# Depthwise convolutions of a two-block network: matrix multiplies replaced by multiply-add instructions on VectorE

## The chip, the cores and the metric

The kernel runs as one program on one core of a Trainium2 chip. The core has a matrix engine (TensorE, PE in the profile), a vector engine (VectorE, DVE), a scalar engine (ScalarE, ACT), GpSimd (POOL) and SyncE (SP), whose queue issues nearly all transfers here. The engines run beside each other, each through its own list of instructions in a fixed order, and wait for each other on semaphores. The metric is the device time of one execution in microseconds (us), as the median of three runs.

## The reference

A state-space block over 256 tokens of width 1024 is followed by a two-layer block that works on two streams, the tokens `x` and a context of 256 tokens. The mixer of each layer has four branches: a Fourier mix, a convolution, grouped attention and differential attention. The convolution is the part that matters here; it is depthwise over tokens, 31 taps wide, on 512 channels:

```python
def conformer_conv(z, w, bias, ln_g, ln_b):
    a, g = jnp.split(z, 2, axis=-1)
    u = a * jax.nn.sigmoid(g)
    pad = CONV_KERNEL // 2                      # CONV_KERNEL = 31
    y = lax.conv_general_dilated(u, w[:, None, :], window_strides=(1,), padding=[(pad, pad)],
                                 dimension_numbers=("NWC", "WIO", "NWC"), feature_group_count=512) + bias
    return jax.nn.silu(layer_norm(y, ln_g, ln_b))
```

It is needed three times: in layer 0 for the context and for `x`, in layer 1 for `x` alone (the context is not updated in the last layer).

## The kernel before

Activations lie with the features on the 128 partitions and the 256 tokens along the free dimension. All large products are made in three multiplies of a rounded high part and a low part: for every weight tile, `wunits` loads 128x1024 values (`ws`), ScalarE casts them to the high part `wh` (L336), VectorE subtracts to get the low part `wl` (L337), and `mm3` (L358) issues 24 multiplies of 128x128 by 128x256 for it. There are four buffers each of `wh` and `wl`, so the split of a weight tile waits until TensorE has freed the buffer of an earlier one.

`conv_start` (L1043) makes the first half of the convolution branch. For each of four groups of 128 channels it multiplies the two input projections, and forms the gated input `up` with one ScalarE and one VectorE instruction (L1057, L1058), between zeros that POOL writes (L1054, L1055). The padded rows then go to DRAM (`du`) and come back as `ux`, a tile that holds 32 channels in four copies, each shifted by one token. With a table of diagonal 32x32 blocks (`cw`, loaded from `w_cv`), 32 matrix multiplies of 128x32 by 32x256 (L1070) sum the taps four at a time, and ScalarE adds the bias and writes `cy` (L1072). `conv_steps` (L1075) takes `cy` later: its first instruction, L1080, adds the four groups for the layer norm.

The calls are: L1701 for the context of layer 0, inside the first block; L1712 for `x` of layer 0, ahead of its `mixer`; L1739 for `x` of layer 1. In `mixer` (L1469) come the projections, grouped attention (`gqa_steps`), differential attention with the Fourier mix and the first gated branches beside it, and only then `conv_steps`, beside the branch `zd`. A softmax (L1295) is a chain of VectorE and ScalarE steps: the maximum of the scores (L1299), its scaling (L1300), the exponential on ScalarE (L1302), the reciprocal of the sum (L1304), the scaling of the probabilities (L1332 or L1368), which TensorE then transposes (L1312).

The order on each engine is made when the program is built. A list scheduler gives every instruction a priority, by default the place in which the code issues it, and puts those that are ready on their engines by priority. `high_priority(offset=...)` shifts the priority of what is issued inside it; a negative offset moves it back by so many places. The kernel has used that for the second block's modulation weights (`ada_next`, L973).

Of the kernel before, what the change touches and what calls it, by code (L numbers as in the profile page):

```python
# [9 lines left out]
F32 = mybir.dt.float32  # L10
F32R = mybir.dt.float32r
I32 = mybir.dt.int32
AF = mybir.ActivationFunctionType
ALU = mybir.AluOpType
# [3 lines left out]
P = 128  # L18
D = 1024
L = 256  # L20
# [11 lines left out]
def _vec_layout():  # L32
    off = 0
    for name, n in (
        ("norm_ffn", 8), ("norm_ple", 8), ("norm_final", 8), ("final_norm", 8),
        ("norm_mix2", 16), ("norm_ffn2", 16), ("b_ada", 96), ("c", 16),
        ("conv_b", 8), ("ln_g", 8), ("ln_b", 8), ("diff_norm", 2),
        ("qn", 128), ("kn", 128),
    ):
        VEC[name] = (off, n)  # L40
        off += n
    return off


NVEC = _vec_layout()

S5C = {}
# [17 lines left out]
def _cols(v):  # L65
    return np.asarray(v).reshape(-1, P).T


def _wfeat(w, cols_per_unit=1):

    k, m = w.shape
    return w.reshape(k // P, P, m // P, P).transpose(2, 1, 0, 3)


def host_layout(i):
    a = {k: np.asarray(v) for k, v in i.items()}
    o = {}
# [10 lines left out]
    def put(name, v, at=0):  # L88
        off, n = VEC[name]
        vec[:, off + at : off + at + v.shape[1]] = v  # L90
# [10 lines left out]
    put("ln_g", _cols(a["conv_ln_g_2"]))  # L101
    put("ln_b", _cols(a["conv_ln_b_2"]))
    put("diff_norm", a["diff_norm_2"].T)
    lam = np.stack([a["lam_q1_2"], a["lam_k1_2"], a["lam_q2_2"], a["lam_k2_2"]], axis=1)
    o["lam"] = np.broadcast_to(lam.reshape(1, 512), (P, 512))
    put("qn", np.broadcast_to(a["q_norm_2"].reshape(1, 128), (P, 128)))
# [51 lines left out]
    o["w_ada1"] = a["w_ada_2"][1].reshape(4, 2, P, 12, 512).transpose(3, 0, 2, 1, 4).reshape(48, P, 1024)  # L158
    wc = [_wfeat(w_in[l][:, 512:1536]).reshape(2, 4, P, 1024).transpose(1, 2, 0, 3) for l in range(2)]
    o["w_cin"] = np.stack(wc).reshape(8, P, 2048)  # L160

    cw = np.concatenate([a["conv_w_2"], np.zeros((2, 1, 512), np.float32)], axis=1).reshape(2, 8, 4, 4, 4, 32)
    cv = np.zeros((2, 4, 4, 32, 8, 4, 32), np.float32)
    e = np.arange(32)
    cv[:, :, :, e, :, :, e] = cw.transpose(5, 0, 3, 2, 1, 4)
    o["w_cv"] = cv.reshape(8, P, 1024)
    tok = np.concatenate([w_in[:, :, 0:512], w_in[:, :, 1536:3840]], axis=2)

    o["w_tok"] = tok[:, :, 1024:1280].reshape(2, 8, P, 256).transpose(0, 2, 1, 3).reshape(2, P, 2048)
# [18 lines left out]
    for l in range(2):  # L188
        w = _wfeat(a["w_ffn2_2"][l])
        for part in range(2):  # L190
            v = w[:, :, part * 8 : part * 8 + 8].reshape(4, 2, P, 1024)
# [9 lines left out]
    e = np.arange(64)  # L201
    an = 2.0 * np.pi * ((e[:, None] * e[None, :]) % 64) / 64
    bd = np.zeros((2, P, P))
    for h in range(2):
        q = slice(64 * h, 64 * h + 64)
# [78 lines left out]
class Net:  # L284
# [758 lines left out]
    def conv_start(self, l, h):  # L1043


        V, S, G, T = self.V, self.S, self.G, self.T
        y = self.k4([P, 4, L], F32, "cy")
        for k in range(4):
            ua, ug = self.wunits(self.a["w_cin"][l * 4 + k])
            ps = self.pm((P, 2, L))  # L1050
            self.mm3(ps[:, 0], ug, h, range(KC))
            self.mm3(ps[:, 1], ua, h, range(KC))
            up = self.up.tile([P, CW], F32, tag="up", bufs=2, name=self.nm("up"))
            G.memset(up[:, 0:15], 0.0)  # L1054
            G.memset(up[:, L + 15 : CW], 0.0)  # L1055
            t = self.k1([P, L])
            S.activation(t, ps[:, 0], AF.Tanh, scale=0.5)  # L1057
            V.scalar_tensor_tensor(up[:, 15 : 15 + L], t, 1.0, ps[:, 1], op0=ALU.add, op1=ALU.mult)  # L1058
            out = self.dr.tile([P, CW], F32, tag="du", name=self.nm("du"))
            self.nc.sync.dma_start(out, up)  # L1060
            sh = self.up.tile([P, 4, L + 28], F32, tag="ux", name=self.nm("ux"))
            v = out.rearrange("(q c) s -> c q s", c=32)
            for i in range(4):
                self.nc.sync.dma_start(sh[32 * i : 32 * i + 32], v[:, :, i : i + L + 28])
            w = self.k4([P, 8, 4, 32], F32, "cw")
            self.nc.sync.dma_start(w.rearrange("p j q c -> p (j q c)"), self.a["w_cv"][l * 4 + k])
            ps = self.px()
            for j in range(8):
                for q in range(4):
                    T.matmul(ps[32 * q : 32 * q + 32, :], w[:, j, q], sh[:, q, 4 * j : 4 * j + L],  # L1070
                             start=j == 0, stop=j == 7)
            S.activation(y[:, k], ps, AF.Identity, bias=self.cb2[:, l * 4 + k : l * 4 + k + 1])  # L1072
        return y

    def conv_steps(self, l, y, z):  # L1075
# [536 lines left out]
    def run(self):  # L1612
        tc, nc = self.tc, self.nc
        V, S, G = self.V, self.S, self.G
        with ExitStack() as st:
            def pool(name, bufs=1, es=st, **k):
                return es.enter_context(tc.tile_pool(name=name, bufs=bufs, **k))
# [3 lines left out]
            self.p1 = pool("p1")  # L1621
            self.p2 = pool("p2")
            self.p4 = pool("p4")
            self.dr = pool("dr", 2, space=bass.MemoryType.DRAM)
            self.psm = pool("psm", 3, space=PSUM)
            self.psx = pool("psx", space=PSUM)
            self.vecs = self.c.tile([P, NVEC], F32, name="vecs")
# [47 lines left out]
            gm, gf, cy, nl = [], [], [], []  # L1675
# [55 lines left out]
            k = self.gqa_kv(ckv, 1, hc1[0], False)  # L1731
# [23 lines left out]


NH = 6
CW = L + 32
ADA_OFF = 50
R_GQA = 0.75  # L1760
R_DIFF = 0.7
# [20 lines left out]
```

## Time and profile before

| | before |
|---|---|
| median of 3 runs | 2021.85 us (2019.74 to 2024.06) |
| profiled execution, time | 2019.47 us |
| profiled execution, span from first to last instruction | 2017.7 us |
| mean granted TensorE clock | 0.984 |
| TensorE busy | 1941.5 us, 96% |
| VectorE busy | 1418.4 us, 70% |
| ScalarE busy | 930.7 us, 46% |
| GpSimd busy | 129.2 us, 6% |

The profile is of one execution, taken instruction by instruction. The busy time of an engine is the time that at least one of its instructions was running; instructions of one engine overlap a little, so what an instruction costs its engine is the distance from its start to the next one's, not its duration. The chain that ended last is followed back from the last instruction, at each step to what released it. A stretch is given in microseconds from the first instruction. The profiled execution's own time, 2019.47 us, is 1.8 us more than its span, which is what lies around the instructions.

### The profile page before, as it was taken

How to read it: one execution, taken by the hardware profiler on the slowest of the kernel's cores; microseconds unless marked ns; L12 is line 12 of the kernel's file. 1: busy time of each engine (PE TensorE's matmuls, PEld its weight loads, DVE VectorE, ACT ScalarE, POOL GpSimd, SP SyncE). 2: the span in 40 equal slices, each digit the busy share in tenths (PEclk: the TensorE clock that was granted, in tenths of full speed). 3: DMA queues.
4: the chain of work that ended last, by engine and by line, in shares of the span. 5: the costliest groups of instructions: out<-in, count | busy, mean ns of one | idle time of the engine just before them, and what ended most of it. 6: DMA issues, size and time to landing. Idle time of an engine off the chain costs nothing.

```text
span 2017.7 us, 36900 instructions
## 1 busy us (share of the span) xinstructions
PE 1941.5 (96%) x14610; PEld 1705.7 (85%) x14610; DVE 1418.4 (70%) x2761; ACT 930.7 (46%) x1595; POOL 129.2 (6%) x156
## 2 busy tenths in 40 slices
PE   3869999999999999999999999999999999999998
PEld 1557899998789997789998777787987789999997
DVE  9974577657667775878878577675766776766665
ACT  2443445545765553764553222222454664544443
POOL 6720000000000010000000000000100000010000
PEclk8879999999999999999999999999999999999999
DMA  5666665575345567236665355453566235565663
GB/s 176 181 200 233 215 208 184 186 219 159 113 141 173 180 207 220 88 95 209 190 190 160 116 168 162 153 162 107 153 195 205 71 110 161 185 194 158 187 185 109
DMA packets 113564, 338.45 MB, mean 168 GB/s; under 512 B 17568, under 2 KB 27568, under 8 KB 113008
## 3 DMA queue, kind: packets, MB, share of 16 engines
q1 hardware_dynamic: 112624, 334.44, 53.0%
q8 instruction: 115, 1.88, 0.4%
q0 software_dynamic: 336, 1.44, 0.2%
q14 instruction: 57, 0.47, 0.1%
q10 hardware_dynamic: 432, 0.21, 0.0%
HBM read 330.61 MB, written 2.82 MB: 165 GB/s over the span
## 4 chain that ended last, share of the span: by engine, by line
PE 89%; DVE 6%; DMA 2%; issue 1%; ACT 1%; POOL 0%; SPq 0%; DVEq 0%; ACTq 0%; POOLq 0%
PE pm L368 21%; PE pm L369 21%; PE pm L370 21%; PE pm L1035 3%; PE pm L1034 3%; PE pm L1036 3%; PE px L1070 2%; PE px L1363 1%; PE px L1312 1%; PE px L923 1%; PE pm L377 1%; PE pm L378 1%; PE pm L379 1%; PE px L1345 1%; PE px L409 1%
## 5 line engine op out<-in xcount | busy, mean ns | idle before, releaser
L337 DVE TENSOR_TENSOR wl<-ws,wh 128x1024 fp32r<-128x1024 f32 (+3 forms) x556 | 613.8, 1114 | 357.8 <-ACT wh L336 353.8
L336 ACT CAST wh<-ws 128x1024 fp32r<-128x1024 f32 (+3 forms) x556 | 532.3, 959 | 720.7 <-PE pm L369 393.8
L368 PE MATMUL pm<-h,wh 128*128 128x256 f32 (+1 forms) x928 | 302.0, 325 | 0.0
L369 PE MATMUL pm<-h,wh 128*128 128x256 f32 (+1 forms) x928 | 301.2, 325 | 0.0
L370 PE MATMUL pm<-h,wl 128*128 128x256 f32 (+1 forms) x928 | 298.3, 321 | 0.0
L368 PE MATMUL pm<-m,wh 128*128 128x256 f32 (+1 forms) x704 | 213.7, 304 | 0.0
L369 PE MATMUL pm<-m,wh 128*128 128x256 f32 (+1 forms) x704 | 213.2, 303 | 0.0
L370 PE MATMUL pm<-m,wl 128*128 128x256 f32 (+1 forms) x704 | 212.6, 302 | 0.0
L368 PEld LDWEIGHTS pm<-h,wh 128*128 128x128 f32 x928 | 175.3, 189 | 22.9 <-ACT wh L336 4.6
L370 PEld LDWEIGHTS pm<-h,wl 128*128 128x128 f32 x928 | 175.9, 190 | 15.6
L369 PEld LDWEIGHTS pm<-h,wh 128*128 128x128 f32 x928 | 175.5, 189 | 14.9 <-issue 0.8
L368 PE MATMUL pm<-hx,wh 128*128 128x256 f32 x640 | 181.6, 284 | 0.0
L369 PE MATMUL pm<-hx,wh 128*128 128x256 f32 x640 | 178.2, 278 | 0.0
L370 PE MATMUL pm<-hx,wl 128*128 128x256 f32 x640 | 177.9, 278 | 0.0
L434 POOL TENSOR_TENSOR ssq<-ssq,sq 128x256 f32<-128x256 f32 x45 | 43.3, 962 | 1656.1 <-ACT sq L428 1654.7
L368 PEld LDWEIGHTS pm<-m,wh 128*128 128x128 f32 x704 | 134.5, 191 | 8.5 <-ACT wh L336 1.7
L369 PEld LDWEIGHTS pm<-m,wh 128*128 128x128 f32 x704 | 134.5, 191 | 6.7 <-issue 1.7
L370 PEld LDWEIGHTS pm<-m,wl 128*128 128x128 f32 x704 | 134.5, 191 | 4.9
L957 DVE SCALAR_TENSOR_TENSOR ac<-wa,sc,ac 128x512 f32<-128x512 f32 x168 | 116.6, 745 | 28.6 <-DMA wa<-w_ada 28.6
L368 PEld LDWEIGHTS pm<-hx,wh 128*128 128x128 f32 x640 | 120.4, 188 | 1.6 <-issue 1.3
L369 PEld LDWEIGHTS pm<-hx,wh 128*128 128x128 f32 x640 | 120.6, 188 | 1.1 <-issue 0.8
L370 PEld LDWEIGHTS pm<-hx,wl 128*128 128x128 f32 x640 | 120.6, 188 | 0.7 <-issue 0.7
(440 smaller groups left out, 4217.4 us busy)
## 6 DMA issues: line engine op xcount, KB each, us to landing
wa<-w_ada SPq DMA_DIRECT2D x96, 512.0 KB, 4.1
ws<-w_gp SPq DMA_DIRECT2D x96, 512.0 KB, 3.6
ws<-w_f SPq DMA_DIRECT2D x88, 512.0 KB, 4.4
ws<-w_tok SPq DMA_DIRECT2D x76, 512.0 KB, 4.6
ws<-mlp_w SPq DMA_DIRECT2D x64, 512.0 KB, 3.8
ws<-w_gp SPq DMA_DIRECT2D x96, 256.0 KB, 2.7
ws<-w_f2a SPq DMA_DIRECT2D x32, 512.0 KB, 4.1
ws<-w_cin SPq DMA_DIRECT2D x24, 512.0 KB, 4.7
```

Of the source, the lines that this page charges most:

```text
L336: self.S.copy(hi, src)
L337: self.V.tensor_tensor(lo, src, hi.bitcast(F32), op=ALU.subtract)
L368: self.T.matmul(out, h, ah, start=start and i == 0, stop=False)
L369: self.T.matmul(out, h, al, start=False, stop=False)
L370: self.pe_last = self.T.matmul(out, l, ah, start=False, stop=stop and i == n - 1)
L377: self.T.matmul(out, wh, act.hi(k), start=k == 0, stop=False)
L434: (eng or self.G).tensor_tensor(acc, acc, sq, op=ALU.add)
L957: V.scalar_tensor_tensor(acc[:, v], st[:, i], c, acc[:, v], op0=ALU.mult, op1=ALU.add)
L1034: self.T.matmul(ps, hi, a, start=k == 0, stop=False)
L1035: self.T.matmul(ps, lo, a, start=False, stop=False)
L1036: self.pe_last = self.T.matmul(ps, hi, b, start=False, stop=k == KC - 1)
L1070: T.matmul(ps[32 * q : 32 * q + 32, :], w[:, j, q], sh[:, q, 4 * j : 4 * j + L], start=j == 0, stop=j == 7)
```

## The change

The matrix multiplies of L1070, the way through DRAM, the shifted copies, the table `w_cv` and the ScalarE evictions are gone. The 31 taps of each channel are put into the table of vectors instead (`conv_w`, 248 columns more). `conv_start` now keeps all four groups of a call in one `up` tile, and then issues for each group one `tensor_scalar` (first tap times input, plus bias) and 30 `scalar_tensor_tensor` (tap times the input shifted by one more token, plus what is summed so far), all on VectorE and all in place in `cy`. These 124 instructions per call stand in a `high_priority` with offset -1200, behind everything that the code issues in the next 1200 places.

```diff
-        ("conv_b", 8), ("ln_g", 8), ("ln_b", 8), ("diff_norm", 2),
+        ("conv_b", 8), ("ln_g", 8), ("ln_b", 8), ("diff_norm", 2), ("conv_w", 248),
...
-        V, S, G, T = self.V, self.S, self.G, self.T
-        y = self.k4([P, 4, L], F32, "cy")
+        V, S, G = self.V, self.S, self.G
+        up = self.up.tile([P, 4, L + 30], F32, tag="up", name=self.nm("up"))
+        G.memset(up[:, :, 0:15], 0.0)
+        G.memset(up[:, :, L + 15 : L + 30], 0.0)
         for k in range(4):
             ua, ug = self.wunits(self.a["w_cin"][l * 4 + k])
             ps = self.pm((P, 2, L))
             self.mm3(ps[:, 0], ug, h, range(KC))
             self.mm3(ps[:, 1], ua, h, range(KC))
-            up = self.up.tile([P, CW], F32, tag="up", bufs=2, name=self.nm("up"))
-            G.memset(up[:, 0:15], 0.0)
-            G.memset(up[:, L + 15 : CW], 0.0)
             t = self.k1([P, L])
             S.activation(t, ps[:, 0], AF.Tanh, scale=0.5)
-            V.scalar_tensor_tensor(up[:, 15 : 15 + L], t, 1.0, ps[:, 1], op0=ALU.add, op1=ALU.mult)
-            out = self.dr.tile([P, CW], F32, tag="du", name=self.nm("du"))
-            self.nc.sync.dma_start(out, up)
-            sh = self.up.tile([P, 4, L + 28], F32, tag="ux", name=self.nm("ux"))
-            v = out.rearrange("(q c) s -> c q s", c=32)
-            for i in range(4):
-                self.nc.sync.dma_start(sh[32 * i : 32 * i + 32], v[:, :, i : i + L + 28])
-            w = self.k4([P, 8, 4, 32], F32, "cw")
-            self.nc.sync.dma_start(w.rearrange("p j q c -> p (j q c)"), self.a["w_cv"][l * 4 + k])
-            ps = self.px()
-            for j in range(8):
-                for q in range(4):
-                    T.matmul(ps[32 * q : 32 * q + 32, :], w[:, j, q], sh[:, q, 4 * j : 4 * j + L],
-                             start=j == 0, stop=j == 7)
-            S.activation(y[:, k], ps, AF.Identity, bias=self.cb2[:, l * 4 + k : l * 4 + k + 1])
+            V.scalar_tensor_tensor(up[:, k, 15 : 15 + L], t, 1.0, ps[:, 1], op0=ALU.add, op1=ALU.mult)
+        y = self.k4([P, 4, L], F32, "cy")
+        with self.tc.high_priority(offset=-CONV_OFF):
+            for k in range(4):
+                w = self.vec("conv_w", (l * 4 + k) * 31, 31)
+                b = self.cb2[:, l * 4 + k : l * 4 + k + 1]
+                V.tensor_scalar(y[:, k], up[:, k, 0:L], w[:, 0:1], b, op0=ALU.mult, op1=ALU.add)
+                for i in range(1, 31):
+                    V.scalar_tensor_tensor(y[:, k], up[:, k, i : i + L], w[:, i : i + 1], y[:, k], op0=ALU.mult, op1=ALU.add)
         return y
...
-CW = L + 32
+CONV_OFF = 1200
```

Line numbers after the change are 5 to 12 lower: L332 is the split of before's L337, L1052 the `up` of L1058; L1058 and L1060 are the new instructions; L1287, L1288, L1292 and L1320 are the softmax steps of L1299, L1300, L1304 and L1332.

The order of VectorE at the `up` writes of the call for `x` in layer 0. `wl` are low parts of weights. Before:

```order
L1058 SCALAR_TENSOR_TENSOR up_8960<-k_1596_8963,pm_8911 128x256
L337 TENSOR_TENSOR wl_9232<-ws_9229,wh_9231 128x1024
L337 TENSOR_TENSOR wl_9238<-ws_9235,wh_9237 128x1024
L1058 SCALAR_TENSOR_TENSOR up_9070<-k_1609_9073,pm_9021 128x256
L337 TENSOR_TENSOR wl_9342<-ws_9339,wh_9341 128x1024
L337 TENSOR_TENSOR wl_9348<-ws_9345,wh_9347 128x1024
L1058 SCALAR_TENSOR_TENSOR up_9180<-k_1622_9183,pm_9131 128x256
```

After:

```order
L1052 SCALAR_TENSOR_TENSOR up_8839<-k_1576_8903,pm_8854 128x256
L1058 TENSOR_SCALAR cy_9098<-up_8839,vecs,cb_1572 128x256
L1060 SCALAR_TENSOR_TENSOR cy_9098<-up_8839,vecs,cy_9098 128x256 x2
L332 TENSOR_TENSOR wl_9037<-ws_9034,wh_9036 128x1024
L1060 SCALAR_TENSOR_TENSOR cy_9098<-up_8839,vecs,cy_9098 128x256 x4
L332 TENSOR_TENSOR wl_9043<-ws_9040,wh_9042 128x1024
L1052 SCALAR_TENSOR_TENSOR up_8839<-k_1584_8967,pm_8918 128x256
L1060 SCALAR_TENSOR_TENSOR cy_9098<-up_8839,vecs,cy_9098 128x256
L1058 TENSOR_SCALAR cy_9098<-up_8839,vecs,cb_1572 128x256
```

Between two writes of `up` there were two splits; now six to eight convolution instructions stand there as well.

The order of VectorE in the grouped attention of the same call, some way into its softmaxes (`sm` and `p` are a softmax's sums and probabilities, `px` its scores). Before:

```order
L1299 TENSOR_REDUCE sm_9779<-px_9774 128x1
L1332 TENSOR_SCALAR p_9736<-p_9736,sm_9738 128x512
L1300 TENSOR_SCALAR sm_9779<-sm_9779,qn_9631 128x1
L337 TENSOR_TENSOR wl_10076<-ws_10073,wh_10075 128x1024
L1304 RECIPROCAL sm_9785<-sm_9780 128x1
L1299 TENSOR_REDUCE sm_9800<-px_9795 128x1
L1332 TENSOR_SCALAR p_9783<-p_9783,sm_9785 128x512
L1300 TENSOR_SCALAR sm_9800<-sm_9800,qn_9631 128x1
L1304 RECIPROCAL sm_9806<-sm_9801 128x1
L1299 TENSOR_REDUCE sm_9866<-px_9861 128x1
```

After:

```order
L1287 TENSOR_REDUCE sm_9663<-px_9658 128x1
L1320 TENSOR_SCALAR p_9620<-p_9620,sm_9622 128x512
L1288 TENSOR_SCALAR sm_9663<-sm_9663,qn_9515 128x1
L1060 SCALAR_TENSOR_TENSOR cy_9098<-up_8839,vecs,cy_9098 128x256 x3
L1292 RECIPROCAL sm_9669<-sm_9664 128x1
L1287 TENSOR_REDUCE sm_9684<-px_9679 128x1
L1320 TENSOR_SCALAR p_9667<-p_9667,sm_9669 128x512
L1288 TENSOR_SCALAR sm_9684<-sm_9684,qn_9515 128x1
L1060 SCALAR_TENSOR_TENSOR cy_9098<-up_8839,vecs,cy_9098 128x256 x3
L1292 RECIPROCAL sm_9690<-sm_9685 128x1
```

Between the scaled maximum and the reciprocal stood a split or nothing; now three convolution instructions stand there where no split does.

The order of TensorE at the first convolution group of the same call. Before:

```order
L370 MATMUL pm_9241<-hx_8651,wl_9232 128x256
L368 MATMUL pm_9241<-hx_8651,wh_9231 128x256
L1070 MATMUL px_8975<-ux_8968,cw_8973 32x256 x32
L369 MATMUL pm_9241<-hx_8653,wh_9231 128x256
L370 MATMUL pm_9241<-hx_8651,wl_9232 128x256
L368 MATMUL pm_9241<-hx_8876,wh_9231 128x256
```

After:

```order
L365 MATMUL pm_9046<-hx_8592,wl_9037 128x256
L363 MATMUL pm_9046<-hx_8592,wh_9036 128x256
L364 MATMUL pm_9046<-hx_8594,wh_9036 128x256
L365 MATMUL pm_9046<-hx_8592,wl_9037 128x256
L363 MATMUL pm_9046<-hx_8817,wh_9036 128x256
```

The 32 multiplies of the convolution are gone from between the multiplies of the projection.

## Rows read from the trace of the kernel before

**Rows 1.** The page: busy shares, and the chain that ended last.

```profile
PE 1941.5 (96%) x14610; PEld 1705.7 (85%) x14610; DVE 1418.4 (70%) x2761; ACT 930.7 (46%) x1595; POOL 129.2 (6%) x156
PE 89%; DVE 6%; DMA 2%; issue 1%; ACT 1%; POOL 0%; SPq 0%; DVEq 0%; ACTq 0%; POOLq 0%
```

**Rows 2.** Stretch: busy us (instructions) of PE, PEld, DVE, ACT, POOL; clock, DMA, GB/s.

```profile
419.70:607.80 188.10, 188.04 (x1413) 157.75 (x1412) 123.03 (x316) 106.84 (x224) 0.64 (x8) 0.99 0.49 152
607.80:648.30 40.50, 40.47 (x349) 40.27 (x350) 28.66 (x64) 19.12 (x31) 0.00 (x0) 1.00 0.54 175
748.70:926.80 178.10, 177.92 (x1326) 145.45 (x1325) 124.21 (x270) 102.50 (x195) 4.15 (x18) 1.00 0.48 146
926.80:968.00 41.20, 41.19 (x355) 40.99 (x355) 36.60 (x77) 19.14 (x31) 0.00 (x0) 1.00 0.65 214
1496.30:1677.70 181.40, 179.66 (x1334) 146.88 (x1333) 119.90 (x263) 103.03 (x195) 0.32 (x4) 1.00 0.45 138
1677.70:1718.10 40.40, 40.39 (x348) 40.19 (x348) 28.58 (x63) 19.11 (x31) 0.00 (x0) 1.00 0.51 167
```

**Rows 3.** Chain in time order: start, us, what; first and last of L1070.

```profile
432.96 3.59 PE px L1070 x64
...
1550.62 3.59 PE px L1070 x64
```

**Rows 4.** VectorE in order of time (start, us, what); durations of L993 (ns).

```profile
11.01 1.32 DVE L461 SCALAR_TENSOR_TENSOR e<-e,e 128x32 f32<-128x32 f32 x6
...
15.02 0.18 DVE L461 SCALAR_TENSOR_TENSOR e<-e,e 128x32 f32<-128x32 f32 x1
15.12 0.18 DVE L490 SCALAR_TENSOR_TENSOR s<-s,s 128x32 f32<-128x32 f32 x1
...
662.01 0.41 DVE L1438 SCALAR_TENSOR_TENSOR k<-k,pm 128x256 f32<-128x256 f32 x1
662.34 0.41 DVE L1104 TENSOR_SCALAR k<-k,lg,vecs 128x256 f32<-128x256 f32 x1
662.66 0.42 DVE L1439 TENSOR_TENSOR acc<-acc,k 128x256 f32<-128x256 f32 x1
...
737.78 1.26 DVE L993 SCALAR_TENSOR_TENSOR hx<-k,mod,hx 128x256 fp32r<-128x256 f32 x3
...
L993 DVE SCALAR_TENSOR_TENSOR hx<-k,mod,hx x16: 465/473/485, 721.1 to 1484.5; 128x256 fp32r<-128x256 f32 x16
```

**Rows 5.** Busy time by stretch: the start and a plain branch.

```profile
0.00:125.00 125.00, 72.69 (x936) 42.30 (x936) 117.66 (x284) 37.42 (x89) 72.97 (x61) 0.84 0.56 171
668.00:720.00 52.00, 52.00 (x451) 52.00 (x449) 37.22 (x60) 27.36 (x44) 0.00 (x0) 1.00 0.65 212
```

**Rows 6.** VectorE in order of time in the grouped attention; all softmax maxima.

```profile
827.51 0.16 DVE L1304 RECIPROCAL sm<-sm 128x1 f32<-128x1 f32 x1 [0.94 <-ACT p L1302]
...
846.63 1.23 DVE L337 TENSOR_TENSOR wl<-ws,wh 128x1024 fp32r<-128x1024 f32 x1 [0.48 <-ACT wh L336]
847.78 0.15 DVE L1304 RECIPROCAL sm<-sm 128x1 f32<-128x1 f32 x1
...
L1299 DVE TENSOR_REDUCE sm<-px 128x1 f32<-128x512 f32 (+1 forms) x96 | 56.2, 586 | 4.4 <-PE px L1330 2.4 <-PE px L1363 1.9
```

**Rows 7.** Who waited for whom: us in total, times, longest.

```profile
ACT wh L336 <- PE pm L369: 393.8, 251, 5.7
DVE wl L337 <- ACT wh L336: 353.8, 291, 6.2
DVE sm L1304 <- ACT p L1302: 34.0, 41, 1.8
```

**Rows 8.** VectorE and POOL in order of time ahead of the first x call.

```profile
735.62 2.23 DVE L991 SCALAR_TENSOR_TENSOR k<-x,g,rx 128x256 f32<-128x256 f32 x3
...
734.91 2.27 POOL L434 TENSOR_TENSOR ssq<-ssq,sq 128x256 f32<-128x256 f32 x2 [3.46 <-ACT sq L428]
```

**Rows 9.** Busy time by stretch around the fall of the clock.

```profile
480.00:490.00 10.00, 10.00 (x44) 8.36 (x44) 7.06 (x37) 1.92 (x3) 0.00 (x0) 0.83 0.39 117
```

More of the change, by code (lines that the diff above doesn't have):

```diff
@@ L103, in host_layout @@
     put("diff_norm", a["diff_norm_2"].T)
+    put("conv_w", a["conv_w_2"].reshape(2, 31, 4, P).transpose(3, 0, 2, 1).reshape(P, 248))
     lam = np.stack([a["lam_q1_2"], a["lam_k1_2"], a["lam_q2_2"], a["lam_k2_2"]], axis=1)
@@ L160, in host_layout @@
     o["w_cin"] = np.stack(wc).reshape(8, P, 2048)
[L162 to L166, printed above, removed]
     tok = np.concatenate([w_in[:, :, 0:512], w_in[:, :, 1536:3840]], axis=2)
@@ L1623, in run @@
             self.p4 = pool("p4")
-            self.dr = pool("dr", 2, space=bass.MemoryType.DRAM)
             self.psm = pool("psm", 3, space=PSUM)
```

## The prediction

> **What bounds the kernel now.** I read the page's busy shares first, then the chain that ended last, then the stretches. TensorE is busy for 96% of the span and VectorE for 70%, and 89% of the chain lies on TensorE [rows 1]. So time that leaves TensorE comes back, and VectorE looks as if it had 600 us to give. The 70% is an average, though, and what matters is VectorE's idle time between the moment a convolution's input is ready and the moment its result is needed. I call the three calls of `conv_start` the context call, the first x call and the second x call. In each the interval runs from the first `up` write (L1058) to the first reader of `cy` (L1080): 419.7 to 648.3, 748.7 to 968.0 and 1496.3 to 1718.1 us. The window rows [rows 2] give each in two parts, up to the place where the convolutions end in the new order and the rest. TensorE is covered almost wholly in all six. VectorE is busy 123.0 + 28.7 = 151.7 of 228.6 us, 124.2 + 36.6 = 160.8 of 219.3, and 119.9 + 28.6 = 148.5 of 221.8. Its idle time there is 76.9, 58.5 and 73.3 us.
>
> **What is removed.** The convolution's matrix multiplies stand on the chain twelve times as a piece of 64 records (32 instructions, each run in two passes) of 3.59 us [rows 3]: 12 x 3.59 = 43.1 us, 14.4 us per call. The first and the last of the twelve are shown. All of it lies on TensorE between multiplies that it runs without a pause, so it is gone from the path, if nothing else becomes late. With it go 72 transfers on SP's queue and the 12 ScalarE evictions of L1072; I cost these at nothing, since ScalarE and the transfers are hidden behind TensorE in these stretches, and a gain from them is within the rounding.
>
> **What is added.** 372 VectorE instructions, 12 `tensor_scalar` and 360 `scalar_tensor_tensor` of 128x256. The before kernel has the same form with a per-partition scalar at L993: one lasts 0.475 us, but three in a row last 1.26 us, so each starts (1.26 - 0.475) / 2 = 0.39 us after the one ahead [rows 4]. The `tensor_scalar` with two per-partition scalars, L1104, starts its successor after 0.32 us [rows 4]. Each output is accumulated in place, so every instruction needs the one before it in its chain. What that costs is seen in the start of the kernel: six dependent instructions of L461 in a row take 1.32 us, (1.32 - 0.18) / 5 = 0.23 us each, while the same line between other work gives way after 0.10 us [rows 4]. A direct successor so pays some 0.12 us more. In the new order the scheduler mixes two chains and other work: I count 42 of the 372 that wait for the instruction directly ahead. So 12 x 0.32 + 360 x 0.39 + 42 x 0.12 = 3.8 + 140.4 + 5.0 = 149 us, 50 us per call. VectorE has to hold 50 us where it had 76.9, 58.5 and 73.3, and TensorE's gain shortens each interval by 14.4.
>
> The Trainium skill speaks against that price: "VectorE: DVE Perf Modes", section "The DRAIN you can't avoid", says that after each VectorE operation the next does not start until the pipeline is empty, semaphore or not. The trace does not agree for work that waits for nothing, since starts lie 0.39 us apart with 0.475 us each [rows 4]; it agrees where one waits for the instruction ahead. By the page the addition would be 360 x 0.475 + 12 x 0.40 = 176 us instead of 149.
>
> **Where it lies.** The order shows the new work in two kinds of place. Behind each `up` stand six to eight convolution instructions and two weight splits: 0.33 (as L1438) + 8 x 0.39 + 2 x 1.15 = 5.7 us [rows 4, 6] of VectorE against two units of 24 multiplies. The plain stretch 668 to 720 runs 451 multiplies in 52 us, 0.115 us each, so the two units take 5.5 us [rows 5]. VectorE is then full, hardly over. In the attention part triples stand between the max scaling (L1300) and the reciprocal (L1304). There VectorE waited 0.94 us for the exponential, or ran a split of 1.15 us and did not wait [rows 6]. A triple is 3 x 0.39 = 1.18 us, so a softmax round loses some 0.2 us where the wait was bare. The fill fits the hole.
>
> **The sum.** No engine is busy all the time. The trace shows what VectorE reaches when it is the limit: 117.7 of the first 125 us, 0.94 [rows 5]. With 50 us more, each interval needs (151.7 + 50) / 0.94 = 214.6 us instead of 228.6, (160.8 + 50) / 0.94 = 224.3 instead of 219.3, and (148.5 + 50) / 0.94 = 211.2 instead of 221.8. That is a gain of 14.0, a loss of 5.0 and a gain of 10.6 us. The first x call is thus the place where VectorE becomes the bound. The 5.0 us need not all be lost. ScalarE's casts wait 393.8 us in all for TensorE to free a weight buffer, and VectorE's splits 353.8 us for the casts [rows 7], so the splits run up to the four buffers ahead, at most 4 x 2.8 = 11 us. VectorE may use up part of that lead before TensorE starves; I take 4 of the 5 us back (bounds 0 and 5). So 14.0 + 10.6 - 1.0 = 23.6 us.
>
> Small terms. VectorE work that reads two tensors at a time as POOL does the same takes twice as long: three of L991 last 2.23 us beside POOL's 2.27, against 1.26 [rows 8]. POOL is busy 4.15 us in the first x stretch and under 0.7 in the others [rows 2], so this costs 0 to 4 us there; the new work is thick beside its rope tables, and I take 1. The clock fell to half for a part of 480 to 490 us (0.83 mean of 2.4 GHz, the rest at 1.2) [rows 9]; ahead of it TensorE ran the last 64 convolution records and narrow column sums. It may now stay up: 0 to 1.7 us, I take 0.5. The table of vectors grows by 248 columns, 127 KB, 0.7 us at the 171 GB/s of the first 125 us [rows 5]; it lies beside VectorE work, 0 to 0.7, I take 0. POOL's memsets go from 24 to 6 and wait for a buffer that was read to the end 140 us earlier: nothing. So 23.6 - 1 + 0.5 = 23 us. The profiled execution took 2019.5 us (span 2017.7), which gives 1996.5; the median of the runs, 2021.9, lies 2.4 us above it, which gives 1999.
>
> **The rivals.**
> 1. The whole gain. If VectorE can be packed fuller than 0.94 and uses up its lead, nothing is late: 2021.9 - 43.1 - 1.7 = 1977. For it: at 1.0 the context interval needs 201.7 us and TensorE 228.6 - 14.4 = 214.2; the second x one 198.5 of 207.4. Against it: the first x interval needs 210.8 and has 204.9.
> 2. VectorE as the bound in all three calls. If each instruction costs its full 0.475 us, a call costs 58.6 us, and the intervals need 223.7, 233.4 and 220.3 us: gains of 4.9 and 1.5, a loss of 14.1. The sum is 7.7 us slower, 2029.5. The mechanism is one price; it decides where the three losses balance the gains, at 56 us per call or 0.45 us per instruction. For it: dependent instructions do cost full length [rows 4]. Against it: only 42 of 372 stand behind their own predecessor. The rule quoted above from the Trainium skill ("VectorE: DVE Perf Modes", "The DRAIN you can't avoid") would give this case.
> 3. A wash by latency. There are 96 softmaxes [rows 6], 32 beside each call; if an inserted convolution instruction that VectorE can't interrupt delays each by 0.45 us on TensorE's path, 96 x 0.45 = 43 us, and nothing is left: 2022. Against it: the rounds with a split in the hole did not wait [rows 6].
> 4. The order doesn't do what it says: low priority might push the work to the end of its interval. The order shows it spread from the first `up` on and done some 40 us ahead of its reader, so this has no chance of its own.
>
> **How the numbers follow.** Chances: the forecast, partly hidden (1985 to 2010) 0.45; the whole gain (1975 to 1985) 0.20; between forecast and wash (2010 to 2018) 0.07; a wash (within 0.2%, about what a measurement of this kernel can tell from no change, 2018 to 2026) 0.10; VectorE-bound (slower) 0.18. So faster 0.72, the same 0.10, slower 0.18. The range from 1977 to 2030 reaches from the whole gain to the full price per instruction, and leaves out some 0.1 at either end. The likeliest case's own range is 1985 to 2010.
>
> **What the profile after would show.** No piece of L1070; TensorE's instructions down by 768 records; VectorE's busy time up by about 145 to 150 us, to some 1565, or by about 175 if rival 2 holds. In the new kernel's convolution line, pairs that start 0.39 us apart. VectorE over 0.9 busy from the first `up` of the first x call to its end, and multiplies there that wait for `wl`, a few us in all; the other two calls without such waits. L1304's wait for the exponential, 34.0 us in all before [rows 7], cut to a third. I am wrong if the convolution instructions take 0.47 us or more from start to start, if TensorE's waits for splits or scaled probabilities sum to over 25 us, or if the clock falls in a stretch where it stood at 1.0.

## The result, and the profile after

The changed kernel takes 1997.5 us (median of 4 runs, 1995.88 to 1998.39) where before took 2021.13 beside it: a ratio of 0.9877, 95% interval 0.9865 to 0.9888. The forecast was 1999. The profiled execution took 1997.63 us, with a span of 1995.9, 21.8 us shorter than before's; the forecast for this difference was 23. The total is right. The terms behind it are not all right, as the calls below show.

Page of the changed kernel: busy time by engine, and the chain that ended last. They answer to [rows 1].

```profile
PE 1906.2 (96%) x13842; PEld 1692.7 (85%) x13842; DVE 1548.6 (78%) x3133; ACT 927.4 (46%) x1583; POOL 130.9 (7%) x138
PE 84%; DVE 11%; issue 2%; DMA 2%; ACT 1%; SPq 0%; DVEq 0%; ACTq 0%
```

The 768 records of L1070 are gone, VectorE has 130.2 us more to do, and its share of the chain has risen from 6% to 11%. Where that lies is seen in the stretches: first the three calls, each from its first `up` to the first reader of `cy` (they answer to [rows 2], both parts of a call in one), then places that are spoken of below. The columns are those of [rows 2].

```profile
420.20:639.20 219.00, 217.52 (x1504) 191.67 (x1503) 194.41 (x504) 124.79 (x251) 0.23 (x2) 1.00 0.45 142
740.40:956.60 216.20, 210.13 (x1441) 183.46 (x1439) 203.67 (x470) 120.77 (x223) 7.08 (x12) 1.00 0.46 141
1484.90:1694.50 209.60, 207.94 (x1429) 182.38 (x1428) 191.69 (x451) 120.26 (x222) 0.00 (x0) 1.00 0.42 130
...
480.00:490.00 10.00, 10.00 (x45) 8.01 (x44) 9.71 (x25) 3.53 (x5) 0.00 (x0) 1.00 0.69 225
...
954.00:958.30 4.30, 0.99 (x9) 0.79 (x8) 2.76 (x8) 1.95 (x3) 0.00 (x0) 0.98 0.61 177
958.30:962.00 3.70, 3.70 (x17) 3.52 (x18) 3.55 (x8) 2.07 (x6) 0.00 (x0) 0.56 0.72 208
990.00:1030.00 40.00, 40.00 (x339) 40.00 (x338) 26.88 (x41) 20.40 (x31) 0.00 (x0) 1.00 0.61 201
```

The calls fell from 228.6, 219.6 and 221.8 us to 219.0, 216.2 and 209.6 (the first x call's reader starts at 968.3 in before's trace). That is 9.6 + 3.4 + 12.2 = 25.2 us. Outside the calls the span grew by 3.4, from 1347.7 to 1351.1. VectorE is busy for 0.89, 0.94 and 0.91 of the calls.

VectorE in order of time in the changed kernel (answers to [rows 4] and [rows 6]):

```profile
757.99 0.43 DVE L1052 SCALAR_TENSOR_TENSOR up<-k,pm 128x256 f32<-128x256 f32 x1
758.32 2.87 DVE L1060 SCALAR_TENSOR_TENSOR cy<-up,vecs,cy 128x256 f32<-128x256 f32 x7
...
828.61 1.27 DVE L1060 SCALAR_TENSOR_TENSOR cy<-up,vecs,cy 128x256 f32<-128x256 f32 x3
829.80 0.16 DVE L1292 RECIPROCAL sm<-sm 128x1 f32<-128x1 f32 x1
...
905.26 1.00 DVE L1060 SCALAR_TENSOR_TENSOR cy<-up,vecs,cy 128x256 f32<-128x256 f32 x2
```

The convolution's group on VectorE (busy us, mean ns | idle ahead of it):

```profile
L1060 DVE SCALAR_TENSOR_TENSOR cy<-up,vecs,cy 128x256 f32<-128x256 f32 x360 | 162.6, 485 | 1.4
```

Two waits of the changed kernel (us in total, times, longest; answer to [rows 7]):

```profile
PE px L1074 <- DVE m L1070: 3.3, 1, 3.3
DVE sm L1292 <- ACT p L1290: 3.2, 6, 1.8
```

Seven instructions in 2.87 us are (2.87 - 0.48) / 6 = 0.40 us from start to start. Two that depend on each other in 1.00 are 0.52 apart; 36 of the 360 show that. The triple at 828.61 fills the softmax's hole, and the reciprocal behind it waits for nothing: its line's waits for the exponential fell from 34.0 us [rows 7] to 3.2, where a third was forecast.

### The profile page after: what moved, and what is told of

The parts are those of the page before. It is cut to its first block, busy times and chain, and to the rows that moved or that the text cites. A ratio compares the mean times of both kernels' runs of the same rounds, so it can differ in the third digit from the quotient of the medians.

```text
span 1995.9 us, 35545 instructions
## 1 busy us (share of the span) xinstructions
PE 1906.2 (96%) x13842; PEld 1692.7 (85%) x13842; DVE 1548.6 (78%) x3133; ACT 927.4 (46%) x1583; POOL 130.9 (7%) x138
## 4 chain that ended last, share of the span: by engine, by line
PE 84%; DVE 11%; issue 2%; DMA 2%; ACT 1%; SPq 0%; DVEq 0%; ACTq 0%
PE pm L363 21%; PE pm L364 21%; PE pm L365 21%; PE pm L1029 2%; PE pm L1031 2%; PE pm L1030 2%; DVE wl L332 2%; PE px L1351 1%; DVE cy L1060 1%; PE px L1300 1%; PE pm L372 1%; PE pm L373 1%; PE px L918 1%; PE pm L374 1%; PE px L1333 1%
## 5 line engine op out<-in xcount | busy, mean ns | idle before, releaser
L332 DVE TENSOR_TENSOR wl<-ws,wh 128x1024 fp32r<-128x1024 f32 (+3 forms) x556 | 616.5, 1116 | 267.0 <-ACT wh L331 264.5
L365 PEld LDWEIGHTS pm<-h,wl 128*128 128x128 f32 x928 | 175.7, 189 | 14.9
L363 PE MATMUL pm<-hx,wh 128*128 128x256 f32 x640 | 184.0, 288 | 0.0
L364 PE MATMUL pm<-hx,wh 128*128 128x256 f32 x640 | 180.6, 282 | 0.0
L1060 DVE SCALAR_TENSOR_TENSOR cy<-up,vecs,cy 128x256 f32<-128x256 f32 x360 | 162.6, 485 | 1.4
L429 POOL TENSOR_TENSOR ssq<-ssq,sq 128x256 f32<-128x256 f32 x45 | 43.2, 960 | 1429.2 <-ACT sq L423 1427.8
```

Source lines behind the costliest of these rows:

```text
L332: self.V.tensor_tensor(lo, src, hi.bitcast(F32), op=ALU.subtract)
L363: self.T.matmul(out, h, ah, start=start and i == 0, stop=False)
L364: self.T.matmul(out, h, al, start=False, stop=False)
L365: self.pe_last = self.T.matmul(out, l, ah, start=False, stop=stop and i == n - 1)
L429: (eng or self.G).tensor_tensor(acc, acc, sq, op=ALU.add)
L1060: V.scalar_tensor_tensor(y[:, k], up[:, k, i : i + L], w[:, i : i + 1], y[:, k], op0=ALU.mult, op1=ALU.add)
```

## The experiments

The theory on trial was that of the prediction: each call is set by how much work VectorE must do in it, and all that TensorE gave up was on the path.

**1. One tap.** How much is the removal worth when VectorE gets almost nothing?

```diff
-                for i in range(1, 31):
+                for i in range(1, 1):
```

> Leaves out 30 of the 31 taps: the 360 scalar_tensor_tensor are gone, the 12 tensor_scalar stay, so the result is not the convolution's. It asks what the removal is worth when VectorE gets almost nothing new. Theory (each call is set by VectorE's capacity between its first `up` and its reader, and all that TensorE gave up was on the path): 2021 - 43.1 for the matrix multiplies - 1.7 for the clock = 1976 us, 1972 to 1980. Rival A (every softmax is delayed by inserted instructions): 1976 too, since nothing is inserted. Rival B (part of the 43 us was never on the path, the rest of the change costs nothing): it stays where the changed kernel is, 1990 to 1998.

Measured: 1982.01 us beside 2020.38 of before, ratio 0.9811 (0.9796 to 0.9826). Stretches of the three calls:

```profile
420.40:634.60 214.20, 214.16 (x1504) 190.89 (x1503) 152.78 (x383) 124.84 (x252) 0.23 (x2) 1.00 0.47 145
736.00:944.00 208.00, 207.86 (x1437) 182.71 (x1436) 160.86 (x351) 120.98 (x223) 4.29 (x12) 1.00 0.47 146
1471.90:1678.80 206.90, 206.45 (x1420) 181.19 (x1419) 148.29 (x331) 120.33 (x222) 0.00 (x0) 1.00 0.42 131
```

TensorE is covered in all three, and they are 14.4, 11.6 and 14.9 us shorter than before: 40.9 of the expected 44.8. So the removed multiplies did lie on the path, which is against rival B, and the new VectorE work takes 15.5 us back. But outside the calls this kernel is 3.3 us longer than before, and its 1982 is 6 us above the sum and 2 above the expected range. Something else had become slower.

**2. Half the taps.**

```diff
-                for i in range(1, 31):
+                for i in range(1, 16):
```

> Leaves out 15 of the 31 taps of each channel (180 of the 360 scalar_tensor_tensor), so VectorE's addition falls from 50 to some 25 us per call. Theory (capacity, a limit that is passed or not): the context call needs (151.7 + 25) / 0.96 = 184 us where TensorE needs 214, the first x call (160.8 + 25) / 0.96 = 194 of 205, the second x call 181 of 207, so nothing is late and the time is that of the one-tap kernel or up to 4 us more: 1976 to 1981. Rival A (delay per inserted piece of work): half the pieces leave half of the 21 us that the changed kernel lost: 1986 to 1989.

Measured: 1992.21 us, ratio 0.9859 (0.9844 to 0.9874). Both expectations missed; the three calls show how:

```profile
420.00:639.00 219.00, 216.33 (x1504) 191.19 (x1503) 173.91 (x443) 125.47 (x251) 0.24 (x2) 1.00 0.45 142
740.30:951.80 211.50, 209.83 (x1433) 182.53 (x1432) 182.34 (x411) 121.38 (x223) 10.56 (x12) 1.00 0.47 144
1479.80:1689.30 209.50, 206.12 (x1413) 179.16 (x1412) 169.58 (x391) 120.02 (x222) 0.00 (x0) 1.00 0.41 128
```

Half the work makes the context call and the second x call as long (219.0, 209.5) as all of it does (219.0, 209.6), with VectorE only 0.79 to 0.81 busy. There it isn't the amount that costs. In the first x call the time rises with it: 208.0, 211.5, 216.2 for one tap, half and all. But that isn't the capacity theory either, a limit that is passed or not: with half the taps VectorE is 0.86 busy there, below any limit that was taken, and the call is already 3.5 us longer. And of the 4.7 us between half and all, 4.4 are idle time of TensorE (6.1 against 1.7 us), 2.9 of which stand behind 906 us, where the convolution is done already: 1.2 at 926 us, and 1.7 of a stop at 954 to 958 us that is spoken of below. No call shows the theory as it was stated.

**3. The first x call on TensorE.** The matrix form of before for this call, with `ux` in the `up` tile's place (288 columns) and the short-lived padded rows in a general buffer:

```diff
+        dve = self.ncall in ON_DVE
...
+            if dve:
+                V.scalar_tensor_tensor(up[:, k, 15 : 15 + L], t, 1.0, ps[:, 1], op0=ALU.add, op1=ALU.mult)
+                continue
...
+ON_DVE = (0, 2)
```

> The first x call (layer 0) goes back to the matrix multiplies and the way through DRAM; the context call and the second x call keep the multiply-adds. Theory (capacity): the first x call gained almost nothing in the changed kernel (its first `up` comes 8.3 us earlier than before, the work behind the call 8.9 us), so the time stays: 1996 to 2001. Rival A (the gain of 23.6 us is spread over the three calls as the softmaxes are): a third is lost, 1997.5 + 7.9 = 2005, 2003 to 2008.

Measured: 2004.01 us, ratio 0.9919 (0.9904 to 0.9933): rival A's number. But this kernel differs in more than the call. Here is a stretch behind the first x call, where TensorE multiplies without a gap at full clock:

```profile
998.00:1038.00 40.00, 40.00 (x335) 40.00 (x335) 27.34 (x41) 20.24 (x32) 0.00 (x0) 1.00 0.59 194
```

It runs 335 multiplies in 40 us, where the changed kernel runs 339 (990 to 1030 above). So the run doesn't compare calls alone; run 11 repeats it on equal terms.

**4. No low priority.** `CONV_OFF = 0`.

> CONV_OFF = 0: the convolution instructions have the priority of their place in the code, so they run as blocks of up to 12, 26 and 49 in a row (4.7, 10 and 19 us) ahead of later weight splits. Theory (TensorE lives on splits that are at most four buffers, 11 us, ahead): the blocks of 15 and 19 us starve it by about 15 us per call beyond the lead, more than the 14.4 us that the call gave: 2020 to 2050. Rival C (the low priority doesn't matter, since VectorE's total is the same): 1995 to 2001.

Measured: 2088.3 us, ratio 1.0338 (1.0321 to 1.0355). The direction is the theory's, the size is more than it had. One block on VectorE, and who waited for splits:

```profile
459.29 19.47 DVE L1060 SCALAR_TENSOR_TENSOR cy<-up,vecs,cy 128x256 f32<-128x256 f32 x49
```

```profile
PE pm L1031 <- DVE wl L332: 50.4, 4, 15.7
PE pm L365 <- DVE wl L332: 30.1, 2, 15.5
```

TensorE stood for 80.5 us in six waits, and the granted clock was 0.93 to 0.95 of 2.4 GHz over the calls, where it had been 1.00:

```profile
420.80:670.00 249.20, 219.00 (x1504) 195.09 (x1503) 199.21 (x504) 124.77 (x251) 0.24 (x2) 0.93 0.41 125
771.30:1015.40 244.10, 214.03 (x1433) 184.70 (x1432) 207.47 (x471) 120.92 (x223) 7.74 (x12) 0.95 0.40 124
1543.20:1785.10 241.90, 212.68 (x1419) 183.98 (x1418) 194.02 (x451) 120.77 (x222) 0.00 (x0) 0.94 0.36 112
```

The same 372 instructions at the same price, 0.40 us ((19.47 - 0.47) / 48), cost some 90 us more in another order (2088.3 against 1997.5). So the low priority is not an accessory of the change; the change would be a loss without it.

**5. Two chains at a time.** The taps of two groups alternate, so that none needs the one directly ahead:

```diff
+            for p in range(0, 4, 2):
+                for i in range(31):
+                    for k in (p, p + 1):
...
```

> The convolution instructions are issued alternately for two channel groups, so that none needs the one directly ahead. In the changed kernel 36 of the 360 started their successor only after 0.52 us instead of 0.40. Theory (capacity): 36 x 0.12 = 4.3 us less on VectorE, of which the first x call, where VectorE is full, hands on its third and the others a part: 1 to 3 us faster than the changed kernel, 1994.5 to 1996.5. But two groups of a pair must be there before it starts, so the work comes some 12 us later: 0 to 3 us slower is the other side. Rival (latency of dependent instructions is hidden between other work): 1997.5.

Measured: 2002.12 us, ratio 0.9898 (0.9881 to 0.9915). Pairs at 0.52 us fell from 36 to 13 and the line's busy time from 162.6 to 158.4 us, and the kernel was no faster, if anything slower: 1.6 us above the slower side of what was expected. Its context and first x call:

```profile
419.50:645.10 225.60, 221.44 (x1504) 195.46 (x1503) 194.24 (x503) 125.39 (x251) 0.23 (x2) 0.98 0.45 138
746.40:959.60 213.20, 209.29 (x1438) 183.35 (x1437) 203.39 (x471) 120.71 (x222) 7.08 (x12) 1.00 0.45 140
```

The first x call became 3.0 us shorter and the context call 6.6 us longer. A pair of chains has fewer dependent instructions and starts later, and this run doesn't separate the two.

**6. The additions of the layer norm early**, in `conv_start`, at its low priority.

```diff
+            m = self.up.tile([P, L], F32, tag="um", name=self.nm("m"))
+            V.tensor_tensor(m, y[:, 0], y[:, 1], op=ALU.add)
+            V.tensor_tensor(m, m, y[:, 2], op=ALU.add)
+            V.tensor_tensor(m, m, y[:, 3], op=ALU.add)
...
```

> The three additions over the channel groups (the first VectorE work of the layer norm) stand directly behind the convolution, at its low priority, in place of the place where the layer norm begins. In the changed kernel TensorE waited 3.3 us for them in the first x call, behind a weight split that waited for a transfer, and then ran 3.7 us at a granted clock of 0.56 (1.6 us). Theory (the order of VectorE, not its capacity, costs these): 3.3 + 1.6 = 4.9 us faster than the changed kernel, 1991 to 1994. Rival (capacity: the additions only move work, the next thing is late instead): within 1.5 us of 1997.5.

Measured: 1999.59 us, ratio 0.9885 (0.9867 to 0.9903), against 0.9877 for the changed kernel: no gain, as the rival says (the time itself is 0.6 us above the rival's range). The wait of 3.3 us for L1070 is gone from the trace, and in its place stands the next step of the same norm:

```profile
PE px L404 <- DVE ssq L429: 3.7, 1, 3.7
```

**7. The modulation products later**, queued behind the mixer's last accumulation.

```diff
+            if self.ada_off == 0 and hasattr(self, "acc_last"):
+                with self.tc.issue_after(self.acc_last.ins):
+                    for _ in range(n):
+                        next(self.todo, None)
+                return
```

> The VectorE products for the second block's modulation weights (18 of them ran at 875 to 950 us, inside the first x call) are queued behind the last accumulation of that mixer. Theory (capacity): the first x call has 18 x 0.67 = 12 us more of VectorE's time, so what it lost behind 875 us comes back in part: 2 to 6 us faster than the changed kernel, 1991.5 to 1995.5. Rival (these products fill time in which VectorE would wait for transfers or casts): within 1 us of 1997.5, or slower if the feed-forward layer behind then waits for them.

Measured: 1996.1 us, ratio 0.9864 (0.9843 to 0.9884). That lies between the two expectations, and its interval overlaps the changed kernel's (0.9865 to 0.9888): a gain of 2 us can't be told from none. The wait for L1070 is gone, and only a new one of 0.8 us for a split is there. The first x call:

```profile
743.40:955.00 211.60, 207.61 (x1421) 181.03 (x1420) 192.44 (x451) 120.66 (x222) 7.07 (x12) 1.00 0.44 134
```

With all its taps it is as long as with half of them (211.6 against 211.5), with VectorE 0.91 busy. But the time outside the calls grew from 1351.1 to 1354.7: most of the 4.6 us only moved.

**8. All three.**

> The three edits of the runs before together: two chains, the additions early, the modulation products later. Theory: the gains add up where they lie in different stretches: 1986 to 1993. Rival: all three buy the same idle time, and the best of them alone is as good: 1991 to 1996.

Measured: 2003.96 us, ratio 0.9905 (0.9889 to 0.9921), worse than either expectation. None of the three edits of VectorE's order brought anything that can be measured, and together they cost some 5 us.

**9. A wider `up` tile.** The 6 us left over in run 1 and the 3.4 us outside the calls pointed to TensorE itself. In the stretch 990 to 1030 us of the changed kernel TensorE runs 339 multiplies at full clock and without a gap. The same work in before:

```profile
1000.00:1040.00 40.00, 40.00 (x347) 40.00 (x346) 27.25 (x41) 20.84 (x32) 0.00 (x0) 1.00 0.63 203
```

That is 347, or 115 ns for one in place of 118. The multiplies concerned have their moving tile (`hx`, `hc`, part of `h`) in a pool that lies behind `up`, and `up` has another size now.

```diff
-        up = self.up.tile([P, 4, L + 30], F32, tag="up", name=self.nm("up"))
+        up = self.up.tile([P, 4, L + 36], F32, tag="up", name=self.nm("up"))
```

> The changed kernel with `up` 292 columns wide in place of 286; nothing else differs, the six columns are never read. The tile's size sets where the pools behind it lie, `hx`, `hc` and a part of `h` among them. In the traces the 128x256 multiplies follow each other by the distance of their moving tile from their weight tile, modulo 128 bytes: before, 64 bytes, median 114 ns, mean 117.3 over 3538; the changed kernel, 96 bytes, 117 and 120.1; the run with the first x call on TensorE, 0 bytes, 120 and 121.2. The wider tile brings the 64 bytes of before back. Theory D (the change slowed these multiplies by moving the tiles): 3538 x 2.8 ns = 9.9 us less on TensorE, so 1987 to 1991. If VectorE is the bound of the calls it takes a part of it back: 1991 to 1994. Rival (the pace comes from something else, such as VectorE's traffic): 1997.5, with medians still at 117.

Measured: 2000.45 us, ratio 0.9889 (0.9872 to 0.9907). Not what theory D said. The stretch of plain work still holds 339:

```profile
990.00:1030.00 40.00, 40.00 (x339) 40.00 (x338) 27.13 (x41) 20.72 (x32) 0.00 (x0) 1.00 0.63 201
```

The multiplies on `hx` have a median of 118 ns, so the rule of the theory (the distance modulo 128 bytes) was wrong, and with it the expectation; whether position matters at all was open again.

**10. One tap, wider `up`.**

> As the one-tap run (leaves out 30 of the 31 taps), with `up` 292 columns wide. That run gained 38.4 us where the sum had 43.1 + 1.7 = 44.8. Theory D: the 6.4 us missing are the slower multiplies on `hx` and `hc`, so they come back: 3538 x 2.8 ns = 9.9 us at most, 1972 to 1977. Rival (the rest of the 43.1 was not on the path): 1980 to 1983.

Measured: 1982.65 us, ratio 0.9802 (0.9788 to 0.9815): no change against run 1, for the same reason.

**11. The first x call on TensorE, wider `up`.**

> As the run with the first x call on TensorE, with the shared `up` tile 292 columns wide, so that it and the wider changed kernel have the same distances between tiles. Its 2004.0 us were read as a third of the gain lost, but its multiplies on `hx` took 120 ns. Theory (capacity: the first x call is worth little on VectorE): 1 to 3 us above the wider changed kernel. Rival A (each call is worth the same): 7 to 8 us above it. By theory D alone it gains 3538 x 3.9 - 662 x 5.7 ns = 10 us on its 2004: 1994.

Measured: 2006.12 us, ratio 0.9918 (0.9904 to 0.9932), on the same chip as run 9: 5.7 us above it. The first x call on VectorE is worth that much, more than capacity alone had it and less than an equal share: neither expectation. (The call itself takes 222.0 us here and 215.2 in run 9.)

**12. 64 bytes ahead of the weights**, beside the wider `up`.

```diff
+            pad = pool("pad")
+            pad.tile([P, 16], F32, tag="pad", name="pad")
             self.wr = pool("wr", 4)
```

> The changed kernel with 64 bytes of padding ahead of the weights' pool and `up` 292 columns wide: now every moving tile, also those of the 4578 multiplies (128x256) that had a distance of 0 and took 120 ns, lies 64 bytes from its weights modulo 128. Theory D: 9.9 us from the first group, 4578 x 3.4 to 6.5 ns = 16 to 30 us from the second, 705 x 3 to 8 ns = 2 to 6 us lost on the 512 columns wide multiplies, which were faster at 0: 1960 to 1975, or up to 10 us more where VectorE becomes the bound. Rival (the distance only stands beside the pace): 1990 to 1998.

Measured: 1980.35 us, ratio 0.9796 (0.9779 to 0.9813), 20.1 us under run 9, which differs from it by 64 unused bytes. It is the fastest kernel of the study that computes the whole. The expected range reaches it only with its allowance for VectorE, and the rule that the range came from (modulo 128 bytes) had failed in run 9: what came true is its part for the multiplies that had a distance of 0. The calls of this run and its plain stretch:

```profile
410.70:629.20 218.50, 215.85 (x1505) 189.75 (x1504) 194.28 (x504) 124.81 (x251) 0.24 (x2) 1.00 0.47 142
729.40:946.10 216.70, 210.19 (x1437) 183.34 (x1435) 203.66 (x470) 120.51 (x223) 5.19 (x12) 0.99 0.45 140
1473.00:1682.00 209.00, 206.80 (x1426) 181.36 (x1424) 191.72 (x451) 120.32 (x222) 0.00 (x0) 1.00 0.43 130
...
980.00:1020.00 40.00, 40.00 (x346) 40.00 (x346) 27.44 (x42) 20.89 (x33) 0.00 (x0) 1.00 0.65 207
```

346 multiplies in 40 us again. And the calls are as long as in the changed kernel (218.5, 216.7, 209.0 against 219.0, 216.2, 209.6): the gain is 16.6 us outside them (1334.5 against 1351.1) and 0.6 inside; against run 9, 19.2 and 1.6. This does not show that VectorE sets the time inside: few of the faster multiplies stand there. Of the 3858 on the tiles `m`, `g`, `y`, `z`, `p`, `zg`, `zd` and `zc` (run 9's trace) 762 do, so that only some 3.5 us could have come back in the calls (an estimate: 299 x 5.2 ns for the last three, 463 x 4.2 ns for the others). What shows that VectorE's new work costs time inside is run 1, which is 4.8, 8.2 and 2.7 us shorter there.

## Why the prediction was right, point by point

Lengths in us, from the traces (before's own spans for comparison):

| | before | predicted | changed | one tap | half the taps | run 12 |
|---|---|---|---|---|---|---|
| context call | 228.6 | 214.6 | 219.0 | 214.2 | 219.0 | 218.5 |
| first x call | 219.6 | 220.3 | 216.2 | 208.0 | 211.5 | 216.7 |
| second x call | 221.8 | 211.2 | 209.6 | 206.9 | 209.5 | 209.0 |
| outside the calls | 1347.7 | 1348.5 | 1351.1 | 1351.0 | 1351.8 | 1334.5 |
| span | 2017.7 | 1994.6 | 1995.9 | 1980.1 | 1991.8 | 1978.7 |

The forecast span is 1.3 us off because its misses cancel: the context call and the time outside took 4.4 and 2.6 us more than forecast, the first and second x calls 4.1 and 1.6 less. That the total came so close is in this part luck; that most of TensorE's 43 us comes back, and VectorE takes a part of it, is the mechanism, and it held.

- **43.1 us on the path.** Right: with one tap the calls lose 40.9 us, and TensorE is covered in them. Against that stand some 5 us by which other multiplies in the calls became slower (the last point). The piece stands on before's chain eleven times, not twelve: at 1536.26 us the chain runs over ScalarE and VectorE beside it. TensorE runs it there all the same, and the second x call lost 14.9 us with one tap.
- **The price, 0.39 us and 0.12 more for a dependent successor.** Right: 0.40 and 0.52, for 36 dependents rather than 42. Rival 2, every instruction at its full duration of 0.485, is out. With it goes what was quoted from the Trainium skill, "VectorE: DVE Perf Modes", section "The DRAIN you can't avoid": in this trace a successor starts some 0.08 us ahead of the end of an instruction that it doesn't need, and waits only for one that it does. The prediction quoted that section by half: it adds that a next instruction which is not held starts earlier, and most of these do start earlier.
- **50 us of VectorE per call.** Too much: its busy time rose by 42.7, 42.6 and 43.2. The convolutions stand in 196 runs between other work, and each run begins under the last 0.08 us of the instruction ahead, which had been counted as busy already: some 16 of the 21 us that were forecast too much over the three calls.
- **Full at 0.94 of the time.** This step failed, and its error covers the last one's. The first x call did reach 0.94, the other two stopped at 0.89 and 0.91. With 43 us and 0.94 the sum would have been 207, 217 and 204, 17 us under what was measured. In the context and second x calls half the work cost the same time, so that capacity is not their limit. Nor did TensorE starve for splits in the first x call, as the sum had it: in none of the three calls does a multiply wait for `wl` (weight loads do so for 0.5 us in all); its longest waits there are those for the norm's sum, 3.3 us, and 1.7 for ScalarE.
- **The first x call as the place that gains least.** Right, though it gained 3.4 us where a loss of 1.0 was forecast. VectorE takes 8.2 of its 11.6 us back, against 4.8 of 14.4 and 2.7 of 14.9 in the others. What was late there is seen at 954 to 958 us: the norm's sum (L1070) stands on VectorE behind a split that waits for a cast, and the casts there for weight transfers, and TensorE does almost nothing for 3.3 us. The convolution had been done since 906 us. The split, and the casts' waits from 940 to 962 us:

```profile
955.68 0.69 DVE L332 TENSOR_TENSOR wl<-ws,wh 128x512 fp32r<-128x512 f32 x1 [1.51 <-ACT wh L331]
ACT wh L331 <- DMA ws<-w_gp: 6.3, 6, 2.2
```

- **Softmaxes (rival 3).** No wash came, but the delay it spoke of is there. From the end of the exponential to the reciprocal it was 0.20 us on average before and 0.25 after, 4.7 us over 96 softmaxes if all of it counted. From the start of the maximum to the end of the reciprocal, though, it was 2.53 before, 2.65 with one tap and 2.86 after (means over the 96 in the traces): 0.21 to 0.33 us per softmax, 20 to 31 us over 96. The calls are 15.7 us longer than with one tap, so not all of this is on TensorE's path; how much is, no run separates.
- **The clock.** 480 to 490 us stands at 1.00 now, where it was 0.83 [rows 9]. But a new fall came where the clock had stood at 1.0, behind TensorE's stop at 954 to 958: a mean of 0.56 over 3.7 us, most of it at 1.2 GHz, which gives back (1 - 0.56) x 3.7 = 1.6 us. The two cancel. This is one of the prediction's own signs of being wrong; its other two did not come.
- **POOL.** The contention fell on POOL, not on VectorE: a table product of 0.30 us took up to 1.30 beside the convolutions, and L1060 never more than 0.564.
- **Not in the sum at all: the multiplies' pace.** The smaller `up` pool moved `hx`, `hc` and part of `h`, and 3440 multiplies went from 115.3 to 118.2 ns, 10 us of TensorE's time. About half of them stand in the calls (1508 of the 2794 on `hx` and `hc`), where with one tap, TensorE being covered, they cost some 5 us (an estimate: 1494 x 3.4 ns); what they cost beside all the taps, no run shows. Outside, the 3.4 us of the table are what is seen of them.

What stays open is what holds the context call and the second x call some 5 and 3 us above TensorE's own time, with half the taps as with all of them. TensorE's bare gaps there are 1.5 and 1.7 us (2.7 and 3.4 with half the taps), spread over many short waits; no single one was found, and the order on VectorE differs between all these kernels. The softmaxes' delay above is a candidate that wasn't tested.

## What to carry to other kernels

Read what an engine has to spare per stretch, between the moment its input is ready and the moment the result is needed, and then test whether the amount of work or its order is what costs: halving the work goes far to answer that in one run. Work that fills another engine's holes wants the lowest priority; here the same instructions at the priority of their place in the code cost some 90 us more. And when a change resizes a buffer, compare the count of identical instructions in a gapless stretch before and after: everything behind that buffer has moved, and its pace may have moved with it.

## What the runs showed of the hardware

How fast 128x256 multiplies follow each other changes with where the moving tile lies against the weight tile. The traces hold no addresses; distances, moving minus weight, modulo 512 bytes, follow from the order and sizes of the pools in the code. The tiles of `hx` and `hc` lie behind the weights' pool (a whole number of 512) and the `up` pool, which has 6848 bytes a partition in before, 4576 in the changed kernel, 4672 in runs 9 and 12 and 4608 in run 3. Spacings are from start to start in the traces, means of those under 153 ns at full clock or nearly so:

| distance, bytes | mean spacing, ns (count) | in |
|---|---|---|
| 0 | 119.5 (4471), 119.5 (4459), 120.1 (4459), 119.9 (7915) | before, changed, run 9, run 3 |
| -32 | 118.2 (3440) | changed |
| 64 | 117.7 (3449), 117.6 (3429) | run 9, run 12 |
| 192 | 115.3 (3454) | before |
| -64 | 114.7 (4459) | run 12 |

Run 9 against run 12 makes a cause of it: 64 bytes of padding took the 4459 multiplies from 120.1 to 114.7 ns, 4459 x 5.4 ns = 24 us, those whose tiles moved together with the weights stayed at 117.7 and 117.6, and the kernel became 20.1 us faster. The 512 columns wide multiplies go the other way: 227.0 ns at a distance of 0 in run 3, where all 1357 of them lie so, and 230.6 to 233.5 at the other distances. Distance alone doesn't give the pace, either. `h` has its rounded high part behind the weights and its low part ahead of them, and in before its last 128x256 multiplies take 118.4 and 116.8 ns on the high part (with `wh` and `wl`), where `hx` at the same 192 bytes takes 114.8; its 512 columns wide ones take 237.6 ns on the low part, at a distance of 0. Why it is so, no run shows; distances other than these five weren't tried, and neither was the 512 (modulo 256, 192 and -64 are the same distance). Run 12 still has 3429 multiplies at 64 bytes, which at 192 or -64 may save another 8 to 10 us of TensorE's time (an estimate: 3429 x 2.3 to 2.9 ns), about half of it inside the calls.
